# The first stretch of a two-layer decoder trunk: weights cut ahead of x, the first tile's products in two passes, copies of x later

## The chip, the cores and the metric

The kernel runs on one core of a Trainium2 chip. The metric is the device time of one execution in microseconds (us). PE is the engine for matrix products and transposes, DVE the vector engine, ACT the scalar engine, POOL a further vector processor, and SP a queue that only issues transfers (DMAs) here. SBUF is the working memory; PE writes its results to PSUM, in banks of 128 x 512 floats.

## What is computed

The reference is a decoder trunk of two layers on 512 positions of width 1024. Layer 0 normalises x, projects it to queries, keys, values and three convolution inputs at once, evaluates a sliding-window attention beside a short gated convolution, and projects both back. Layer 1 has a chunked gated linear attention in its place. Each layer then has a gated feed-forward block with a convolution of width 3, and a gated per-layer embedding. What matters here is the very first step:

```python
h = _rms_norm(x, mix_norm[i])                       # x is 512 x 1024
q, k, v, cb, cc, cx = _split(h @ w_in, HY_SPLITS)   # k and v: 128 columns each
```

Everything is float32. The root mean square is a factor per position, so the kernel projects x times the gain first and multiplies by that factor afterwards.

## The kernel before, in words

**Three products for one.** PE multiplies in a rounded 32-bit format. To keep float32 accuracy, each operand is cut into a high part (rounded) and a low part (the rest), and a product is taken as high x high + high x low + low x high. For x, `split` (line 104) makes the parts: ACT writes the high part a0 with the gain multiplied in (L112), and DVE the low part a1 (L113). For weights, `cut` (line 126) does it: ACT writes wh (L142), DVE wl (L143). `mm3` (line 158) issues the three products: L162 (x high with wh), L163 (x high with wl), L164 (x low with wh).

**Input.** `mixer0` (line 422) loads x in four chunks of 256 columns, each as two transfers `xin[0]` and `xin[1]` (256 positions each), and behind each chunk the matching 256 rows of the key and value weights (`kvr`, 256 columns). All twelve transfers are issued by SP in this order (L433, L433, L434, and again), of 256 KB each. Transfers share eight semaphores, so SP issues the later ones when earlier ones have landed. The weights of the queries (L119) follow on the same queue.

**Order of the first stretch.** x arrives with positions on the partitions, but the products need columns there. So each chunk c is turned by PE: eight transposes of 128 x 128 (L460) into two PSUM tiles `ps`, one for each column tile 2c and 2c+1. `features(c)` does this, then splits both tiles (L112, L113), cuts the chunk's weights (L142, L143), and copies both tiles to `xT` in SBUF, the first on ACT, the second on DVE (L471). `keys_values(k)` multiplies column tile k with the weights: for each of four position blocks the three products of `mm3`, 12 products of 256 columns. They sum up over k = 0..7 in two PSUM tiles `pkv`. In the block under `tc.manual_schedule` PE, DVE and ACT take their instructions in the order in which the program writes them; outside it a scheduler orders them.

The program order is: features(0), keys_values(0), features(1), keys_values(1), features(2), keys_values(2), features(3), keys_values(3) to (7). In `features`, chunk 0 cuts its weights between its two tiles, and the others behind both:

```python
    if m == (c > 0) + 2 * c:
        wkv.append(self.cut(kvr[:, 2 * c : 2 * c + 2, :], "a"))
```

The weights of chunk c (two column tiles) are read by tiles 2c and 2c+1. There are four `ps` tiles; chunk c+2 takes those of chunk c, once all that reads them (split and copies) is done.

**Fills.** `idle(n)` (line 194) issues n products of ones into a PSUM tile that nobody reads (L198). Seven run at the start in `setup`, eight between the transposes of chunk 0 and the first products: `features(0, 8)`.

**Gains.** The gains of the norm arrive as rows and are turned by PE into a column (`vec0`, L222), in the middle of chunk 0's transposes; DVE copies it (L223), and L112 and L113 read it.

**Behind the stretch.** The squares of x for the norm (L486, ACT), the tables of the rotary embedding (from L373 on, DVE), and the query products (L162 to L164 into `ps`, 512 columns) follow.

Of the kernel before, what the change touches and what calls it, by code (L numbers as in the profile page):

```python
# [21 lines left out]
NT = S // P  # L22
ND = D // P
# [33 lines left out]
class Kernel:  # L57
# [364 lines left out]
    def mixer0(self):  # L422
        nc, a, tc = self.nc, self.a, self.tc
        with tc.tile_pool(name="m0", bufs=1) as mp:
# [3 lines left out]
            kvr = self.raw(ND, 256)  # L428
# [10 lines left out]
            xg = self.xg = []  # L439
            tok = lambda k, t: (xg[k][0][:, t * P : (t + 1) * P], xg[k][1][:, t * P : (t + 1) * P])  # L440
            pkv = [self.pa() for _ in range(2)]
            pkv = [pkv[t // 2][:, (t % 2) * 256 : (t % 2) * 256 + 256] for t in range(NT)]
            wkv = []

            def keys_values(k):
                for t in range(NT):
                    self.mm3(
                        pkv[t], tok(k, t), wkv[k // 2](k % 2, 0, 256),
                        start=k == 0 and t % 2 == 0, stop=k == ND - 1 and t % 2 == 1,
                    )  # L450

            def features(c, fill=0):
                ms = (2 * c, 2 * c + 1)
                pss = [self.ps() for _ in ms]
                for u in range(2):
                    if c == 0 and u == 1:
                        self.vec0()
                    for m, ps in zip(ms, pss):
                        for t in (2 * u, 2 * u + 1):
                            nc.tensor.transpose(  # L460
                                ps[:, t * P : (t + 1) * P], xin[u][:, t % 2, m * P : (m + 1) * P], self.ident
                            )
                self.idle(fill)
                for m, ps in zip(ms, pss):
                    hl = self.pair(self.fp, "a0", "a1")
                    self.split(hl, ps, self.g_mix[0][:, m : m + 1])
                    xg.append(hl)
                    if m == (c > 0) + 2 * c:
                        wkv.append(self.cut(kvr[:, 2 * c : 2 * c + 2, :], "a"))
                return [  # L470
                    copy(self.xT[m], ps) for m, ps, copy in zip(ms, pss, (nc.scalar.copy, nc.vector.tensor_copy))  # L471
                ]

            with tc.manual_schedule(engines={ET.PE, ET.DVE, ET.Activation}):
                features(0, 8)
                for c in range(1, 4):
                    keys_values(c - 1)
                    last = features(c)
                for k in range(3, ND):
                    keys_values(k)  # L480
            wq = [self.weights(w_in[:, k0 : k0 + 4, :512], 4, 512, by="a") for k0 in (0, 4)]
            sums = self.few(NT, "ss")
# [174 lines left out]
            pss = {}  # L657
# [101 lines left out]
    def operand(self, m, gain, tags):  # L759


        nc, fp = self.nc, self.mlp
        H = S // 2
        if m % 2 == 0:
            self.scratch = self.four(fp, F32)
        x = self.scratch[:, m % 2]
        nc.scalar.activation(x, self.xT[m], AF.Copy, scale=gain[:, m : m + 1])
        self.xg.append(self.pair(self.fp, *tags))
        self.split(self.xg[m], x)
        if m % 2:  # L770
            e, o, s12, s34 = (self.scratch[:, u] for u in range(4))
            nc.vector.tensor_tensor(s12[:, :H], e[:, H:], o[:, H:], ALU.add)
            nc.vector.tensor_tensor(s12[:, H:], s12[:, :H], e[:, :H], ALU.subtract)
            out = self.four(fp)
            self.split((out[:, 0], out[:, 1]), s12)
            nc.vector.tensor_tensor(s34[:, :H], e[:, :H], e[:, H:], ALU.subtract)
            nc.vector.tensor_tensor(s34[:, H:], o[:, :H], s12[:, H:], ALU.subtract)
            self.split((out[:, 2], out[:, 3]), s34)
            self.forms.append([(out[:, q, c], out[:, q + 1, c]) for q in (0, 2) for c in (slice(0, H), slice(H, S))])
        self.squares(m)  # L780
# [1164 lines left out]
```

## Time and profile before

| what | value |
|---|---|
| time before, median of three runs | 1213.49 us |
| its three runs | 1211.59, 1214.13, 1213.49 us |
| the profiled execution's own time | 1211.17 us |
| its span, first to last instruction | 1209.4 us |
| PE busy | 1201.5 us, 99% of the span |
| DVE, ACT busy | 967.9 and 664.9 us |

A profile is one execution, recorded by the hardware; times in it count from the start of its span. "Busy" is the time in which an engine had an instruction in work. The products on PE are pipelined: one that is recorded with 0.28 us can be followed by the next after 0.12 us, so the distance between two starts is what one costs. PEld is the loading of the stationary operand, which overlaps PE. A row of the timeline has its start, its duration, engine, line, operation, output<-inputs, sizes and count; in brackets stands how long the engine was idle before it, and whom it waited for. In a table of windows the number in brackets is the count of instructions that run in the window, those that reach into it from before among them.

### The profile page before, as it was taken

What the parts mean: (1) busy time and instruction counts of PE and PEld (TensorE: products, weight loads), DVE (VectorE), ACT (ScalarE), POOL (GpSimd) and SP (SyncE); (2) the same over time, 40 slices, a digit from 0 to 9 for tenths busy, and PEclk for the clock granted to TensorE, in tenths of its full rate; (3) what the DMA queues carried; (4) which work ended last, traced back from release to release, by engine and by line L of the source; (5) the groups of instructions that cost most, each with busy time, mean ns of one, the idle gap of its engine ahead of it and who ended that gap; (6) DMA issues with size and microseconds to landing.
All of it is one profiled execution on the core that took longest, in us unless ns stands there. A gap on an engine that the chain in (4) does not pass through costs nothing.

```text
span 1209.4 us, 17733 instructions
## 1 busy us (share of the span) xinstructions
PE 1201.5 (99%) x7030; PEld 1039.7 (86%) x7030; DVE 967.9 (80%) x1529; ACT 664.9 (55%) x1082; POOL 44.5 (4%) x64
## 2 busy tenths in 40 slices
PE   9999999999999999999999999999999999999998
PEld 8877788999899889888988988889998899888877
DVE  6786587899898996746679876687999999978595
ACT  7466465656555644534563555555565555645364
POOL 2600000000000000000100000000000000000000
PEclk9999999999999999999999999999999999999999
DMA  7221322323323242222322222323242424323501
GB/s 221 74 96 43 92 86 70 127 83 105 105 95 115 89 138 97 96 91 91 114 93 70 71 71 70 105 67 108 71 140 70 140 70 131 122 88 106 200 1 70
DMA packets 111271, 117.61 MB, mean 97 GB/s; under 512 B 2856, under 2 KB 106466, under 8 KB 111188
## 3 DMA queue, kind: packets, MB, share of 16 engines
q1 hardware_dynamic: 109824, 115.35, 29.3%
q8 instruction: 55, 0.90, 0.3%
q0 software_dynamic: 560, 0.42, 0.3%
q10 hardware_dynamic: 804, 0.70, 0.2%
q14 instruction: 28, 0.23, 0.1%
HBM read 114.37 MB, written 2.10 MB: 96 GB/s over the span
## 4 chain that ended last, share of the span: by engine, by line
PE 88%; DVE 7%; ACT 2%; issue 1%; POOL 1%; DVEq 0%; ACTq 0%; POOLq 0%
PE ps L162 12%; PE ps L163 12%; PE ps L164 12%; PE pa L163 7%; PE pa L162 7%; PE pa L164 7%; PE ps L848 6%; PE ps L850 5%; PE ps L849 5%; PE pa L848 2%; PE pa L850 2%; PE pa L849 2%; DVE wl L143 1%; PE ps L1345 1%; PE ps L1347 1%
## 5 line engine op out<-in xcount | busy, mean ns | idle before, releaser
L142 ACT ACTIVATE wh<-raw 128x1024 fp32r<-128x1024 f32 (+4 forms) x154 | 152.3, 991 | 152.4 <-PE ps L163 109.3
L143 DVE TENSOR_TENSOR wl<-raw,wh 128x1024 fp32r<-128x1024 f32 (+4 forms) x154 | 175.3, 1140 | 52.9 <-ACT wh L142 52.6
L795 ACT ACTIVATE wh<-raw 128x1024 fp32r<-128x1024 f32 x78 | 82.8, 1061 | 118.3 <-DVE raw L820 65.4
L908 DVE SCALAR_TENSOR_TENSOR zt<-z,vfa,zt 128x510 f32<-128x510 f32 (+1 forms) x176 | 130.9, 746 | 11.7 <-ACT zt L906 11.2
L796 DVE TENSOR_TENSOR wl<-raw,wh 128x1024 fp32r<-128x1024 f32 x78 | 95.4, 1223 | 20.0 <-ACT wh L795 19.9
L906 ACT ACTIVATE zt<-z,vfb 128x512 f32<-128x512 f32 x88 | 71.0, 809 | 29.5 <-DVE four L959 12.8
L162 PE MATMUL ps<-b,wh 128*128 128x512 f32 x192 | 76.8, 400 | 0.0
L163 PE MATMUL ps<-b,wh 128*128 128x512 f32 x192 | 75.2, 392 | 0.0
L164 PE MATMUL ps<-b,wl 128*128 128x512 f32 x192 | 75.0, 391 | 0.0
L163 PE MATMUL pa<-b,wh 128*128 128x512 f32 x176 | 69.0, 392 | 0.0
L163 PE MATMUL pa<-a,wh 128*128 128x512 f32 x176 | 69.0, 392 | 0.0
L162 PE MATMUL pa<-a,wh 128*128 128x512 f32 x176 | 69.0, 392 | 0.0
L162 PE MATMUL pa<-b,wh 128*128 128x512 f32 x176 | 69.0, 392 | 0.0
L164 PE MATMUL pa<-a,wl 128*128 128x512 f32 x176 | 68.5, 389 | 0.0
L164 PE MATMUL pa<-b,wl 128*128 128x512 f32 x176 | 68.5, 389 | 0.0
L848 PE MATMUL ps<-four,wh 128*128 128x256 f32 x232 | 65.2, 281 | 0.4 <-ACT ps L869 0.4
L850 PE MATMUL ps<-four,wl 128*128 128x256 f32 x232 | 64.4, 278 | 0.0
L849 PE MATMUL ps<-four,wh 128*128 128x256 f32 x232 | 64.3, 277 | 0.0
L162 PE MATMUL ps<-a,wh 128*128 128x512 f32 x160 | 63.1, 394 | 0.0
L163 PE MATMUL ps<-a,wh 128*128 128x512 f32 x160 | 62.7, 392 | 0.0
L164 PE MATMUL ps<-a,wl 128*128 128x512 f32 x160 | 62.5, 391 | 0.0
L162 PE MATMUL ps<-uh,wh 128*128 128x512 f32 x128 | 50.3, 393 | 0.0
(469 smaller groups left out, 3504.9 us busy)
## 6 DMA issues: line engine op xcount, KB each, us to landing
raw<-in_ffn_w_up_dram SPq DMA_DIRECT2D x44, 1024.0 KB, 5.0
raw<-in_ffn_w_down_dram SPq DMA_DIRECT2D x13, 1024.0 KB, 4.8
raw<-in_hy_w_in_dram SPq DMA_DIRECT2D x8, 1024.0 KB, 5.1
raw<-in_gla_w_in_dram SPq DMA_DIRECT2D x8, 1024.0 KB, 5.2
raw<-in_ffn_w_down_dram SPq DMA_DIRECT2D x8, 768.0 KB, 4.2
raw<-in_ple_w_gate_dram SPq DMA_DIRECT2D x6, 1024.0 KB, 4.9
raw<-in_hy_w_out_dram SPq DMA_DIRECT2D x16, 256.0 KB, 3.9
raw<-in_gla_w_out_dram SPq DMA_DIRECT2D x4, 1024.0 KB, 4.7
```

The costliest lines, as they stand in the source:

```text
L142: nc.scalar.activation(hv, v, AF.Copy)
L143: nc.vector.tensor_tensor(lv, v, hv.bitcast(F32), ALU.subtract)
L162: mm(out, lh, rh, start=start, stop=False, **kw)
L163: mm(out, lh, rl, start=False, stop=False, **kw)
L164: mm(out, ll, rh, start=False, stop=stop, **kw)
L795: nc.scalar.activation(h, src, AF.Copy)
L796: nc.vector.tensor_tensor(l, src, h.bitcast(F32), ALU.subtract)
L848: mm(out, wh, xh, start=first and j == 0, stop=False, **kw)
L849: mm(out, wh, xl, start=False, stop=False, **kw)
L850: mm(out, wl, xh, start=False, stop=j == ND // 2 - 1, **kw)
L906: nc.scalar.activation(y, z, AF.Identity, scale=w2[:, f : f + 1], bias=bb[:, f : f + 1])
L908: nc.vector.scalar_tensor_tensor(out=y[:, tap:], in0=z[:, : S - tap], scalar=w[:, f : f + 1], in1=y[:, tap:], op0=ALU.mult, op1=ALU.add,)
```

## The change

The order inside the first stretch is written anew. `features` is gone; its parts are now four small functions, and tile 0 has products of its own:

```diff
-            def features(c, fill=0):
-                ms = (2 * c, 2 * c + 1)
-                pss = [self.ps() for _ in ms]
+            def first_keys_values():
+                mm = nc.tensor.matmul
+                wh, wl = wkv[0](0, 0, 256)
+                for t in range(NT):
+                    xh, _ = tok(0, t)
+                    mm(pkv[t], xh, wh, start=t % 2 == 0, stop=False)
+                    mm(pkv[t], xh, wl, start=False, stop=False)
+                for t in range(NT):
+                    mm(pkv[t], tok(0, t)[1], wh, start=False, stop=False)
+
+            def turned_in(c):
+                pss = [self.ps() for _ in range(2)]
                 for u in range(2):
                     if c == 0 and u == 1:
                         self.vec0()
...
-                self.idle(fill)
-                for m, ps in zip(ms, pss):
-                    hl = self.pair(self.fp, "a0", "a1")
-                    self.split(hl, ps, self.g_mix[0][:, m : m + 1])
-                    xg.append(hl)
-                    if m == (c > 0) + 2 * c:
-                        wkv.append(self.cut(kvr[:, 2 * c : 2 * c + 2, :], "a"))
+                return pss
+
+            def weight(c):
+                wkv.append(self.cut(kvr[:, 2 * c : 2 * c + 2, :], "a"))
+
+            def operand(m, ps):
+                hl = self.pair(self.fp, "a0", "a1")
+                self.split(hl, ps, self.g_mix[0][:, m : m + 1])
+                xg.append(hl)
+
+            def keep(c, pss):
                 return [
-                    copy(self.xT[m], ps) for m, ps, copy in zip(ms, pss, (nc.scalar.copy, nc.vector.tensor_copy))
+                    copy(self.xT[2 * c + u], pss[u]) for u, copy in enumerate((nc.scalar.copy, nc.vector.tensor_copy))
                 ]
 
             with tc.manual_schedule(engines={ET.PE, ET.DVE, ET.Activation}):
-                features(0, 8)
+                pss = turned_in(0)
+                self.idle(3)
+                weight(0)
+                for u in range(2):
+                    operand(u, pss[u])
+                first_keys_values()
                 for c in range(1, 4):
-                    keys_values(c - 1)
-                    last = features(c)
-                for k in range(3, ND):
+                    ahead = turned_in(c)
+                    keep(c - 1, pss)
+                    pss = ahead
+                    operand(2 * c, pss[0])
+                    weight(c)
+                    operand(2 * c + 1, pss[1])
+                    keys_values(c)
+                last = keep(3, pss)
+                for k in range(4, ND):
                     keys_values(k)
```

What it does, in the order of the instructions:

- Three fills stand behind chunk 0's transposes, where there were eight.
- On ACT and DVE the weights of chunk 0 are cut ahead of both x tiles of the chunk; before, they stood between the two.
- Tile 0's products come in two passes: for all four position blocks the two with a0, then for all four the one with a1. Before, the three products of a block stood together.
- For chunks 1 to 3 the weights are cut between the chunk's two x tiles; before, they stood behind both.
- The copies of x to `xT` of chunk c stand behind the transposes of chunk c+1 in the program, and ahead of its splits. On ACT and DVE that is behind chunk c's splits and cuts and ahead of chunk c+1's, the place that they had; those of chunk 3 stand behind its products.
- PE's order of transposes and products by tiles is that of before: chunk 0, tile 0, chunk 1, tile 1, chunk 2, tile 2, chunk 3, tiles 3 to 7.

More of the change, by code (lines that the diff above doesn't have):

```diff
@@ L457, in features @@
                         self.vec0()
-                    for m, ps in zip(ms, pss):
+                    for m, ps in zip((2 * c, 2 * c + 1), pss):
                         for t in (2 * u, 2 * u + 1):
@@ L462, in features @@
                             )
-                self.idle(fill)
-                for m, ps in zip(ms, pss):
-                    hl = self.pair(self.fp, "a0", "a1")
-                    self.split(hl, ps, self.g_mix[0][:, m : m + 1])
-                    xg.append(hl)
-                    if m == (c > 0) + 2 * c:
-                        wkv.append(self.cut(kvr[:, 2 * c : 2 * c + 2, :], "a"))
+                return pss
[6 more added lines that the diff above has]
+            def keep(c, pss):
                 return [
-                    copy(self.xT[m], ps) for m, ps, copy in zip(ms, pss, (nc.scalar.copy, nc.vector.tensor_copy))
+                    copy(self.xT[2 * c + u], pss[u]) for u, copy in enumerate((nc.scalar.copy, nc.vector.tensor_copy))
                 ]
             with tc.manual_schedule(engines={ET.PE, ET.DVE, ET.Activation}):
-                features(0, 8)
-                for c in range(1, 4):
-                    keys_values(c - 1)
-                    last = features(c)
-                for k in range(3, ND):
+                pss = turned_in(0)
[4 more added lines that the diff above has]
+                first_keys_values()
+                for c in range(1, 4):
+                    ahead = turned_in(c)
[7 more added lines that the diff above has]
+                for k in range(4, ND):
                     keys_values(k)
```

## The prediction

> **What bounds the kernel now.** I read the page first, then the waits of PE, then the first 45 us by windows, and last the timeline of PE, ACT, DVE and SP there. The page's busy line and the waits of PE (engine, line, what it waited for; us in total, times, longest):
>
> ```profile
> span 1209.4 us, 17733 instructions
> ...
> PE 1201.5 (99%) x7030; PEld 1039.7 (86%) x7030; DVE 967.9 (80%) x1529; ACT 664.9 (55%) x1082; POOL 44.5 (4%) x64
> ```
>
> ```profile
> PE pa L198 <- DVE mhalf L186: 1.3, 1, 1.3
> PE pa L163 <- DVE wl L1325: 0.9, 1, 0.9
> PE ps L1345 <- ACT so L1389: 0.5, 1, 0.5
> PE pa L629 <- ACT pT L637: 0.5, 1, 0.5
> PE ps L848 <- ACT ps L869: 0.4, 2, 0.2
> PE ps L162 <- DVE kT L1532: 0.2, 1, 0.2
> PE pa L163 <- DVE wl L143: 0.2, 1, 0.2
> ```
>
> PE is busy 99% of the span and waits 4.0 us in all, so the time is the length of PE's own list. A cut counts if it takes instructions off that list or ends a hole in it early on, and if what follows really moves up. But busy isn't useful: the change is about the stretch up to 23.1 us, and there PE also runs L198, products of ones whose result nobody reads. PE's timeline of the start (start, us, ..., count):
>
> ```profile
> 1.32 3.36 PE L198 MATMUL pa<-ones_r 128*128 128x512 f32 x7 [1.32 <-DVE mhalf L186]
> 4.47 1.06 PE L460 MATMUL ps<-cf,xin 128*128 128x128 f32 x4
> 5.46 0.28 PE L222 MATMUL pa<-cf,vrow 16*128 16x16 f32 x1
> 5.67 0.97 PE L460 MATMUL ps<-cf,xin 128*128 128x128 f32 x4
> 6.40 2.08 PE L198 MATMUL pa<-ones_r 128*128 128x512 f32 x8
> 8.31 0.28 PE L162 MATMUL pa<-wh,a 128*128 128x256 f32 x1
> 8.53 0.39 PE L163 MATMUL pa<-wl,a 128*128 128x256 f32 x1
> 8.75 0.28 PE L164 MATMUL pa<-wh,a 128*128 128x256 f32 x1
> ```
>
> Start to start, the first seven fills take (4.47-1.32)/7 = 0.45 us each, the eight from 6.40 on (8.31-6.40)/8 = 0.24: PE's clock doubles at about 6.4, although the granted clock reads 1.00 from the start (I take that for missing records). The same stretch by windows (stretch and length, PE busy and count, PEld, DVE, ACT, POOL, PEclk, DMA):
>
> ```profile
> 8.30:9.94 1.64, 1.64 (x13) 1.42 (x12) 1.43 (x3) 0.36 (x1) 0.00 (x0) 1.00 1.07 374
> 9.94:10.73 0.79, 0.79 (x10) 0.79 (x9) 0.00 (x0) 0.00 (x0) 0.00 (x0) 1.00 1.09 385
> 10.73:12.25 1.52, 1.52 (x15) 1.52 (x14) 0.73 (x2) 1.45 (x3) 0.19 (x2) 1.00 1.09 398
> 13.04:14.98 1.94, 1.76 (x15) 1.57 (x14) 1.94 (x4) 1.89 (x5) 1.94 (x4) 1.00 0.83 287
> 15.77:23.14 7.37, 7.37 (x63) 7.24 (x61) 5.51 (x9) 7.27 (x12) 2.96 (x6) 1.00 0.69 157
> 23.14:45.20 22.06, 22.06 (x98) 18.21 (x98) 14.31 (x40) 11.72 (x23) 6.58 (x6) 1.00 0.38 116
> ```
>
> The list reads: products of tile 0 (1.64), transposes of chunk 1 (0.79), tile 1 (1.52), transposes of chunk 2 (0.79, to 13.04), tile 2 (1.94), transposes of chunk 3, then tiles 3 to 7 (7.37). Twelve products cost 1.52 when nothing holds them; tile 2's row has 0.42 more: the wait for wl, below.
>
> **The change part by part.** PE's order stays, transposes of chunk c and then products of tile c, but for five fills fewer and tile 0's inner order; behind 23.1 us PE, POOL and SP have the same lists as before, DVE and ACT swap a few neighbours up to about 33 us. So there are two places to price.
>
> *Five fills off, and the weights ahead of x.* ACT and DVE at the start (idle before, and its releaser, in brackets), and SP's tenth and eleventh transfers:
>
> ```profile
> 6.40 0.69 ACT L112 ACTIVATE a<-ps,vec 128x512 fp32r<-128x512 f32 x1 [3.17 <-PE ps L460]
> 6.99 0.62 ACT L142 ACTIVATE wh<-raw 128x512 fp32r<-128x512 f32 x1
> 7.51 0.68 ACT L112 ACTIVATE a<-ps,vec 128x512 fp32r<-128x512 f32 x1
> 8.08 0.58 ACT L471 COPY xT<-ps 128x512 f32<-128x512 f32 x1
> ```
>
> ```profile
> 7.12 0.75 DVE L113 SCALAR_TENSOR_TENSOR a<-ps,vec,a 128x512 fp32r<-128x512 f32 x1 [1.17 <-ACT a L112]
> 7.79 0.68 DVE L143 TENSOR_TENSOR wl<-raw,wh 128x512 fp32r<-128x512 f32 x1
> ```
>
> ```profile
> 5.84 0.47 SPq L433 DMA_DIRECT2D xin<-in_x_dram  x1
> ```
>
> The fills run until 8.31, but the operand a0 is done at 6.40+0.69 = 7.09, so they hold PE back; the second product starts at 8.53 since wl is done only at 7.79+0.68 = 8.47. In the changed order wh goes first on ACT and adds a wait there, for the first weight transfer; the x operands stand behind it. SP's transfer at 5.84 waits, by the program, for the lane of that weight transfer, so it had landed by 5.84. Then wh runs 5.88 to 6.50; a product operand follows a wh after 0.52 (6.99 to 7.51), so at 6.40: ACT is ready when x is, and the move costs nothing. Its cover is 0.0 us wide, though: each us that the weights land later delays a0 by as much. wl on DVE runs 6.52 to 7.20, a1 at 7.12 as before. Three fills end at 6.40 + 3 x 0.24 = 7.12. So the first product starts at about 7.2 with wh and wl both there, and twelve products (1.5; the four with a1 stand last, a1 is done at 7.87) bring chunk 1's transposes to 8.7 instead of 9.94: **1.25 us** less. From both sides: 1.19 if only the five fills count (5 x 0.24), 1.35 if the first product starts at 7.10.
>
> *wl of the second weight chunk.* PE around 13.04, and what led there on ACT and DVE:
>
> ```profile
> 13.04 0.36 PE L162 MATMUL pa<-wh,a 128*128 128x256 f32 x1
> 13.58 0.39 PE L163 MATMUL pa<-wl,a 128*128 128x256 f32 x1 [0.17 <-DVE wl L143]
> ```
>
> ```profile
> 10.80 1.27 ACT L112 ACTIVATE a<-ps,vec 128x512 fp32r<-128x512 f32 x2 [2.14 <-PE ps L460]
> 11.95 0.64 ACT L142 ACTIVATE wh<-raw 128x512 fp32r<-128x512 f32 x1
> ```
>
> ```profile
> 11.52 1.41 DVE L113 SCALAR_TENSOR_TENSOR a<-ps,vec,a 128x512 fp32r<-128x512 f32 x2 [1.79 <-ACT a L112]
> 12.84 0.68 DVE L143 TENSOR_TENSOR wl<-raw,wh 128x512 fp32r<-128x512 f32 x1
> 13.44 0.68 DVE L471 COPY xT<-ps 128x512 f32<-128x512 f32 x1
> ```
>
> Now wl is third on DVE (two a1, 11.52 to 12.84) and ends at 13.52; PE stands until 13.58. Afterwards it is second. By the same steps from the transposes' start T = 8.7: first operand at T + 0.86 (9.94 to 10.80), wh 0.59 later, a1 at T + 1.58, wl 0.67 behind it, done at T + 2.93 = 11.6. PE asks for it at T + 0.79 + 1.52 + 0.79 + 0.2 = 12.0. It is there 0.4 us early, so the wait goes: **0.42 us** (1.94 - 1.52). If that margin is eaten, up to 0.42 comes back.
>
> *What is late next.* The copies of x now stand behind the next transposes in the list; on ACT and DVE they land between operands. Chunk 3's transposes write the tile that the copy of chunk 1 frees: by the steps above that copy ends on DVE at 12.9, asked for at 13.5. The third chunk's wl ends near 14.2, asked for at 15.7; the fourth's near 16.7, asked for at 18.6. All cover, so I cost these at 0; if the nearest failed, it would cost some 0.1 to 0.4. Chunk 1's x must be there at 8.7; SP's 5.84 row has the weight transfer ahead of it done, and its two pieces of 256 KB, at 0.7 us each (374 GB/s in the 8.30 window), then land near 7.3. The next weights (L119) start when DVE has cut the last chunk, so some 1.9 us earlier; nobody loses a place in SP's or POOL's queue.
>
> *Sum.* 1.25 + 0.42 = 1.7 us. Behind 23.1 PE is full (22.06 of 22.06), and the waits from there on are 2.5 us in five rows, each behind work that PE itself began; so the 1.7 us passes to the end, with ACT's and DVE's room there as the cover. At worst, if a chain fixed in time ended last, all of it would be lost; below that I see nothing, since no later list grows.
>
> The profiled execution took 1211.17 us (span 1209.4 and 1.8 around it): 1209.5 after. The three runs lie 0.4 to 3.0 above it, their median 2.3. Off the median 1213.49 the sum gives 1211.8, off the mean of the four executions (1212.6) 1210.9. I take the middle, 1211.4.
>
> **The rivals.** *The clock doubles earlier.* In a run where it opens near 4.5, the eight transposes from 4.47 take about half as long and before gains 0.9: its a0, wh, wl then bring products at 7.5. The changed kernel has wh no earlier than 5.84 and a0 behind it at 6.40, as now. The head start shrinks from 1.25 to 0.3, and with 0.42 the gain is 0.7: 1212.4. For it: the runs differ by 2.5 us, and one record cannot tell where the clock opens. A later opening changes little, as products then run slow in the fills' place.
>
> *Given back later.* ACT and DVE move up less than PE (ACT is busy 7.27 of 7.37 us in the row of 15.77), and a wait behind 23.1 grows by what PE won: 1213. Against: from 23.14 to 45.20 ACT is busy 11.7 of 22.1 us and DVE 14.3, with room to catch up before the attention.
>
> *Slower: the clock stays shut.* The fills may be what opens it. With three instead of eight, and operands that come a little late, PE might run the products at the slow rate until a later opening; each us so run loses half a us (0.45 against 0.24). The gain is gone if it opens 3.4 us behind the first product, at 10.6; at 15.4 us the net is +2.4: 1215.5. Against: in the trace it opens at about 6.4, ahead of the first fill that goes, and the list has no hole over 0.1 us behind it. [...]
>
> **How the numbers follow.** Chances: 0.68 that the 1.7 us shows, 0.14 for 0.7, 0.11 for given back, 0.07 for slower. About 0.2% (2.4 us, 1211.1) is what a measurement of this kernel can tell from no change; 1.7 us lies inside it, and the runs' scatter and the base decide: of the 0.68 some 0.41 falls below 1211.1, of the 0.14 some 0.03. Faster 0.44, same 0.50, slower 0.06. The range goes from the lowest run less 1.7 and 0.5 for scatter, 1209.4, to the highest (1214.13) less 0.7, 1213.4; the slower case is left out.
>
> **What would show it.** Right: three fills from about 6.4, first product at 7.2, chunk 1's transposes at 8.7, no wait of PE on wl before 23 us, and the products' end at 21.4 instead of 23.14; each later stage 1.7 us earlier. Wrong: a0 on ACT behind 6.5 (weights late), a wait on wl at tile 2, products 0.21 us apart (clock shut), or a PE wait behind 23 us that is longer by what was won.

## The result, and the profile after

| | before | after |
|---|---|---|
| median of 20 runs each | 1211.92 us | 1209.94 us |
| lowest to highest | 1210.40 to 1214.53 | 1209.26 to 1211.01 |
| the profiled execution | 1211.17 | 1209.60 |
| its span | 1209.4 | 1207.8 |

The ratio of after to before is 0.9982, 95% interval 0.9976 to 0.9987: faster by 0.18%, or 1.6 to 2.9 us. It is a real gain, and a little under the 0.2% that the prediction took for its bound.

The busy line and PE's waits of the page and trace after:

```profile
span 1207.8 us, 17724 instructions
...
PE 1199.9 (99%) x7025; PEld 1038.0 (86%) x7025; DVE 968.9 (80%) x1529; ACT 665.2 (55%) x1082; POOL 43.8 (4%) x64
```

```profile
PE pa L198 <- DVE mhalf L186: 1.3, 1, 1.3
PE pa L163 <- DVE wl L1349: 0.9, 1, 0.9
PE pa L653 <- ACT pT L661: 0.5, 1, 0.5
PE ps L1369 <- ACT so L1413: 0.5, 1, 0.5
PE ps L872 <- ACT ps L893: 0.5, 2, 0.3
PE ps L162 <- DVE kT L1556: 0.2, 1, 0.2
```

PE is as full as before, with 5 instructions and 1.6 us less. The wait on wl of L143 is gone, and no later wait took its place (line numbers behind the change are 24 higher). PE's timeline of the start:

```profile
4.47 1.06 PE L469 MATMUL ps<-cf,xin 128*128 128x128 f32 x4
5.45 0.28 PE L222 MATMUL pa<-cf,vrow 16*128 16x16 f32 x1
5.67 0.81 PE L469 MATMUL ps<-cf,xin 128*128 128x128 f32 x4
6.23 0.94 PE L198 MATMUL pa<-ones_r 128*128 128x512 f32 x3
7.04 0.39 PE L457 MATMUL pa<-wh,a 128*128 128x256 f32 x1
7.26 0.28 PE L458 MATMUL pa<-wl,a 128*128 128x256 f32 x1
```

ACT and DVE in the same stretch:

```profile
5.37 0.63 ACT L142 ACTIVATE wh<-raw 128x512 fp32r<-128x512 f32 x1 [2.14 <-DMA raw<-in_hy_w_in_dram]
6.29 1.27 ACT L112 ACTIVATE a<-ps,vec 128x512 fp32r<-128x512 f32 x2 [0.29 <-PE ps L469]
7.80 0.59 ACT L484 COPY xT<-ps 128x512 f32<-128x512 f32 x1 [0.24 <-DVE a L113]
```

```profile
6.03 0.69 DVE L143 TENSOR_TENSOR wl<-raw,wh 128x512 fp32r<-128x512 f32 x1
7.01 1.41 DVE L113 SCALAR_TENSOR_TENSOR a<-ps,vec,a 128x512 fp32r<-128x512 f32 x2 [0.29 <-ACT a L112]
```

ACT cuts the weights while PE still turns x; its next idle time ends with PE, so x and not the weights holds a0. The fills are over at about the time at which a0 is done (6.29 + 0.69 = 6.98), and both parts of the weights have been ready since 6.72. The windows after, cut at the same places of the list:

```profile
7.03:8.58 1.55, 1.55 (x13) 1.55 (x13) 1.55 (x3) 1.12 (x2) 0.00 (x0) 1.00 0.97 291
8.58:9.37 0.79, 0.79 (x10) 0.79 (x9) 0.44 (x1) 0.00 (x0) 0.00 (x0) 1.00 1.06 371
9.37:10.88 1.51, 1.51 (x15) 1.51 (x14) 0.72 (x2) 1.44 (x3) 0.00 (x0) 1.00 1.09 375
11.67:13.18 1.51, 1.51 (x15) 1.51 (x14) 1.51 (x3) 1.46 (x4) 1.29 (x7) 1.00 1.07 414
13.97:21.33 7.36, 7.36 (x63) 7.23 (x61) 6.31 (x10) 7.02 (x12) 4.59 (x9) 1.00 0.82 196
```

Chunk 1's transposes start at 8.58 instead of 9.94, tile 2 takes 1.51 instead of 1.94, and the stretch ends at 21.33 instead of 23.14: 1.81 us less.

### The profile page after: what moved, and what is told of

Its sections match the earlier page's. It is cut to its first block, busy times and chain, and to the rows that moved or that the text cites. A ratio compares the mean times of both kernels' runs of the same rounds, so it can differ in the third digit from the quotient of the medians.

```text
span 1207.8 us, 17724 instructions
## 1 busy us (share of the span) xinstructions
PE 1199.9 (99%) x7025; PEld 1038.0 (86%) x7025; DVE 968.9 (80%) x1529; ACT 665.2 (55%) x1082; POOL 43.8 (4%) x64
## 4 chain that ended last, share of the span: by engine, by line
PE 85%; DVE 9%; ACT 2%; issue 1%; DMA 1%; POOL 1%; ACTq 0%; DVEq 0%; POOLq 0%
PE ps L162 12%; PE ps L163 12%; PE ps L164 12%; PE pa L163 6%; PE pa L162 6%; PE pa L164 6%; PE ps L872 5%; PE ps L874 5%; PE ps L873 5%; PE pa L872 2%; PE pa L874 2%; PE pa L873 2%; DVE wl L143 2%; PE ps L1369 1%; PE ps L1371 1%
## 5 line engine op out<-in xcount | busy, mean ns | idle before, releaser
L143 DVE TENSOR_TENSOR wl<-raw,wh 128x1024 fp32r<-128x1024 f32 (+4 forms) x154 | 175.8, 1142 | 49.6 <-ACT wh L142 49.1
```

The costliest lines, as they stand in the source:

```text
L143: nc.vector.tensor_tensor(lv, v, hv.bitcast(F32), ALU.subtract)
```

## The experiments

The theory: the gain is a head start of some 1.25 us that needs the fills off and the weights ahead together, and 0.42 us of a wait for wl at tile 2; both pass through to the end. The rivals: each fill is worth its own length; the order on ACT and DVE alone is the gain; the clock needs the fills; what is won is given back later.

Two things move the traces by more than some of these effects. One is the moment at which PE's clock doubles (in e7 products of 256 columns start 0.21 us apart ahead of it and 0.12 behind), which differs from run to run; the column "clock" is the first record of the full clock in each trace. The other is the part behind 23 us. So the comparisons use places in the list. All in us; "c1" is the start of chunk 1's transposes, "c2 to c3" the distance from chunk 2's to chunk 3's (transposes and tile 2), "end" the transpose of the positions (L375), the first instruction behind the key and value products, and "rest" the time from there to the start of the last product. The times given below for e1 to e10 are medians of eleven runs each.

| kernel | clock | first product | c1 | c2 to c3 | end | rest |
|---|---|---|---|---|---|---|
| before | 6.36 | 8.31 | 9.94 | 2.74 | 23.15 | 1182.4 |
| before again (e11) | 6.49 | 8.37 | 9.94 | 2.76 | 23.15 | 1182.3 |
| before again (e12) | 7.29 | 8.77 | 10.19 | 2.74 | 23.39 | 1182.3 |
| after | 6.02 | 7.04 | 8.59 | 2.30 | 21.34 | 1182.6 |
| after again (e10) | 6.84 | 7.40 | 8.83 | 2.30 | 21.58 | 1182.5 |
| e1, three fills only | 4.55 | 6.93 | 9.23 | 2.76 | 22.45 | 1182.2 |
| e2, weights first only | 4.58 | 7.55 | 8.98 | 2.75 | 22.19 | 1183.0 |
| e3, wl late again | 4.35 | 6.87 | 8.44 | 2.74 | 21.64 | 1182.5 |
| e4, one pass | 5.71 | 6.89 | 8.98 | 2.31 | 21.75 | 1182.2 |
| e5, eight fills | 6.60 | 8.45 | 9.88 | 2.30 | 22.63 | 1183.1 |
| e6, no fills behind chunk 0 | 4.61 | 6.86 | 8.41 | 2.31 | 21.19 | 1183.4 |
| e7, no fills at the start | 9.05 | 7.52 | 9.64 | 2.31 | 22.41 | 1182.4 |
| e8, five at the start | 7.41 | 7.47 | 8.91 | 2.30 | 21.66 | 1182.5 |
| e9, six at the start, one later | 4.42 | 6.83 | 8.41 | 2.30 | 21.17 | 1182.3 |

**e1, fills alone.**

```diff
-                features(0, 8)
+                features(0, 3)
```

> The order of before with three fills instead of eight. My theory: the fills only covered the wait for the first weights. The first product then waits for wh (6.99 + 0.62 = 7.6 us) and the second for wl (8.47 us), so chunk 1's transposes still start at 9.85 to 9.95 us, tile 2's wait for wl stays, and the time is that of before (ratio 0.9999 to 1.0001). Rival, each fill is worth its own length: five fills less give 1.2 us, transposes at 8.8 us, ratio 0.999. Rival, the fills hold the clock open: products at 0.21 us each and later than before.

Measured: 1211.04 us, ratio 0.9996 (0.9987 to 1.0005). PE at its first products, and the DVE row that ends the wait:

```profile
5.61 0.94 PE L198 MATMUL pa<-ones_r 128*128 128x512 f32 x3
6.93 0.38 PE L162 MATMUL pa<-wh,a 128*128 128x256 f32 x1 [0.38 <-ACT wh L142]
7.80 0.39 PE L163 MATMUL pa<-wl,a 128*128 128x256 f32 x1 [0.49 <-DVE wl L143]
```

```profile
7.07 0.68 DVE L143 TENSOR_TENSOR wl<-raw,wh 128x512 fp32r<-128x512 f32 x1
```

and ACT ahead of it:

```profile
5.68 0.69 ACT L112 ACTIVATE a<-ps,vec 128x512 fp32r<-128x512 f32 x1 [2.45 <-PE ps L460]
6.26 0.62 ACT L142 ACTIVATE wh<-raw 128x512 fp32r<-128x512 f32 x1
```

The fills' place is taken by waits, first for wh and then for wl, so the fills covered them. The times expected were those of a late clock; here it opened at 4.55, x was turned sooner, and the whole chain with it. Eight fills from 5.61 on, of 0.24 each (e2 has them from 5.62 to 7.55), would have ended near 7.5, still ahead of the 7.80 at which wl lets the second product go: so with an early clock the kernel before should stand at 9.23 and 22.45 too. No run of before had an early clock, so that is worked out and not measured. The times alone do not exclude the 0.999 of the rival that prices each fill at its length, since the interval begins at 0.9987; the waits in the trace speak against it.

**e2, weights first alone.**

```diff
+                if c == 0:
+                    wkv.append(self.cut(kvr[:, :2, :], "a"))
                 for m, ps in zip(ms, pss):
...
-                    if m == (c > 0) + 2 * c:
+                    if c and m == 1 + 2 * c:
```

> The order of before with the first weights cut ahead of both x tiles, and all eight fills. My theory: the eight fills hold PE until 8.3 us whatever is ready, so only the short wait of the second product goes: transposes of chunk 1 at 9.8 us, 0.1 us won, ratio 0.9999. Rival, the order on ACT and DVE is the whole gain: transposes at 8.7 us, ratio 0.999.

Measured: 1211.43 us, ratio 1.0 (0.9991 to 1.0009).

```profile
5.62 2.09 PE L198 MATMUL pa<-ones_r 128*128 128x512 f32 x8
7.55 0.28 PE L162 MATMUL pa<-wh,a 128*128 128x256 f32 x1
7.67 0.28 PE L163 MATMUL pa<-wl,a 128*128 128x256 f32 x1
```

No product waits, but the fills last until 7.55. The 9.8 us expected for c1 was that of a late clock; against e1, where it opened as early, c1 is 0.25 earlier. With the same early clock e6, which has the weights first, the two passes and no fills, reaches its first product at 6.86 and c1 at 8.41, 0.57 earlier than e2 and 0.82 earlier than e1. So neither half brings the head start alone; both single-cause rivals fall in the traces. The 0.57 needs the two passes as well: e4 below has the weights first, three fills and one pass, DVE starts its a1 as early as in e6 (6.87 in both), and its c1 is that of e2, 8.98.

**e3, the later weights behind both x tiles again** (chunks 1 to 3).

```diff
                     operand(2 * c, pss[0])
-                    weight(c)
                     operand(2 * c + 1, pss[1])
+                    weight(c)
```

> The changed kernel with the weights of chunks 1 to 3 behind both x tiles again. My theory: the wait of tile 2's second product on wl comes back, 0.35 to 0.45 us, tile 2 takes 1.9 us instead of 1.5, and the query products start that much later than in the changed kernel; about 0.4 us of its gain is lost (ratio to before 0.9985 instead of 0.9982, inside the noise of the times). Rival, the wait was not on the path: nothing moves behind tile 2.

Measured: 1209.69 us, ratio 0.9986 (0.9978 to 0.9995), in the times not to be told from the change. In the trace the wait is back:

```profile
11.54 0.36 PE L162 MATMUL pa<-wh,a 128*128 128x256 f32 x1
12.07 0.39 PE L163 MATMUL pa<-wl,a 128*128 128x256 f32 x1 [0.17 <-DVE wl L143]
```

The distance of starts is 0.53 where the change has 0.20 at that place, c2 to c3 is 2.74 against 2.30, and the end stands at 21.64; e6, with nearly the same clock and c1, ends at 21.19. The 0.44 us is on PE's list and stays there.

**e4, tile 0 in one pass.**

```diff
-                first_keys_values()
+                keys_values(0)
```

> The changed kernel with tile 0's products in one pass, three for each block as before. My theory: the third product waits for a1, done on DVE at 7.77 us, instead of starting at 7.38; with the restart of the pipeline chunk 1's transposes start 0.4 to 0.55 us later than in the changed kernel (9.0 to 9.15 us instead of 8.59), and stay so to the end of the stretch. Rival, the two passes are worth nothing, because the weights ahead already make all three ready: transposes at 8.6 us.

Measured: 1209.95 us, ratio 0.9986 (0.9977 to 0.9995).

```profile
7.12 0.28 PE L163 MATMUL pa<-wl,a 128*128 128x256 f32 x1
7.68 0.39 PE L164 MATMUL pa<-wh,a 128*128 128x256 f32 x1 [0.28 <-DVE a L113]
```

The third product waits for a1, as expected: 0.56 us from start to start where the two passes have 0.12. From first product to c1 it takes 2.09 us against 1.55 in the change. The two passes are worth 0.5 us, a part of the head start that the prediction had inside its 1.5 for twelve products.

**e5, eight fills in the changed order.**

```diff
-                self.idle(3)
+                self.idle(8)
```

> The changed kernel with eight fills again. My theory: PE is held until 8.2 to 8.3 us, so the first product starts there and chunk 1's transposes at 9.7 to 9.8; of the 1.2 us of head start 1.15 is lost, the 0.42 us at tile 2 stays: ratio to before about 0.9995. Rival, fills behind chunk 0 cost nothing: as the changed kernel.

Measured: 1210.92 us, ratio 0.9996 (0.9987 to 1.0005). Against the changed kernel with nearly the same clock (e10) the first product is 1.05 later, and the end 1.05 too: once the weights are ahead, five fills cost nearly their length (0.25 each here, eight from 6.44 to 8.45, so 1.26).

**e6, no fills behind chunk 0.**

```diff
-                self.idle(3)
+                self.idle(0)
```

> The changed kernel with no fill at all behind chunk 0's transposes. My theory: the first product waits for a0 at 7.0 to 7.1 us anyway, so PE stands idle for 0.7 us and nothing else moves: same times of all later stages, within 0.1 us. Rival, the fills keep the clock open: the products cost 0.21 us instead of 0.12 for a while and the stretch ends 0.5 us or more later.

Measured: 1210.05 us, ratio 0.9990 (0.9981 to 0.9999).

```profile
5.23 0.65 PE L469 MATMUL ps<-cf,xin 128*128 128x128 f32 x4
6.86 0.39 PE L457 MATMUL pa<-wh,a 128*128 128x256 f32 x1 [0.97 <-ACT a L112]
7.08 0.31 PE L458 MATMUL pa<-wl,a 128*128 128x256 f32 x1
```

PE stands 0.97 us, and from the third on the products start 0.12 us apart (7.23, 7.34, 7.46 and on), the fast rate, as in the change (7.38, 7.50, 7.62). e3, with three fills and as early a clock, has its first product at 6.87: these three fills do nothing here. But the clock had opened at 4.61, ahead of the place of the fills, so this trace cannot say what they do while it is still shut. What a0 waits for here is wh, ahead of it on ACT, and wh for its transfer:

```profile
5.60 0.63 ACT L142 ACTIVATE wh<-raw 128x512 fp32r<-128x512 f32 x1 [2.37 <-DMA raw<-in_hy_w_in_dram]
6.13 1.25 ACT L112 ACTIVATE a<-ps,vec 128x512 fp32r<-128x512 f32 x2
```

**e7, no fills at the start.**

```diff
-            self.idle(7)
+            self.idle(0)
```

> The changed kernel without the seven fills of the start (three stay behind chunk 0). PE then begins with transposes when x is there, at about 3.9 us instead of 4.47. [...]

Measured: 1210.56 us, ratio 0.9994 (0.9985 to 1.0003).

```profile
4.09 1.09 PE L469 MATMUL ps<-cf,xin 128*128 128x128 f32 x4 [4.09 <-DMA xin<-in_x_dram]
...
7.52 0.41 PE L457 MATMUL pa<-wh,a 128*128 128x256 f32 x1
7.73 0.41 PE L458 MATMUL pa<-wl,a 128*128 128x256 f32 x1
...
8.80 0.40 PE L457 MATMUL pa<-wh,a 128*128 128x256 f32 x1
9.01 0.30 PE L458 MATMUL pa<-wl,a 128*128 128x256 f32 x1
9.16 0.65 PE L460 MATMUL pa<-wh,a 128*128 128x256 f32 x4
```

Here the rival mechanism of the shut clock is seen at work: the products follow at 0.21 us until 9.05 and at 0.12 behind. c1 is at 9.64, 0.8 later than with an opening at 6.84 (e10). Without the fills at the start the clock opened 1.8 us later than in any trace of the kernels with all seven (7.29), in this one run. Counted from PE's first work, at 4.09, that is 5.0 us.

**e8 and e9, fewer fills at the start.**

```diff
-            self.idle(7)
+            self.idle(5)      # e8; in e9 6, and idle(1) behind chunk 0
```

> The changed kernel with five fills at the start instead of seven. The x of chunk 0 is there at about 3.9 us and at 4.6, but PE's transposes start at 4.47 because seven fills last so long. My theory: transposes start at 3.9, chunk 0's end about 0.5 us earlier, a0 is then held by wh on ACT (done near 6.0): first product near 6.7 instead of 7.04, 0.2 to 0.4 us won if the clock opens as early as now. Rival, the clock opens later with less work ahead of it, and the gain goes.

> The changed kernel with six fills at the start instead of seven and one behind chunk 0 instead of three. The first x is usable at 4.09 us (seen with five fills), and six fills end at 4.04, so the transposes start at 4.09 without the hole that five left. My theory: the first product starts 0.2 to 0.4 us earlier than in the changed kernel for the same opening of the clock, and the stretch ends as much earlier; in the times that is at most 0.03% and not to be told from the changed kernel. Rival: the clock opens later with less work ahead, and it is slower by 0.3 us or more.

Measured: e8 1209.88 us, ratio 0.9993 (0.9984 to 1.0002; the two medians alone give 0.9987, its runs lie between 1209.57 and 1212.0); e9 1209.37 us, 0.9983 (0.9975 to 0.9992). ACT in e9:

```profile
5.57 0.63 ACT L142 ACTIVATE wh<-raw 128x512 fp32r<-128x512 f32 x1 [2.35 <-DMA raw<-in_hy_w_in_dram]
6.11 1.25 ACT L112 ACTIVATE a<-ps,vec 128x512 fp32r<-128x512 f32 x2
```

The transposes do start at 4.07, but wh then waits for its transfer, a0 stands behind it, and c1 comes at 8.41 as in e6: the expected 0.2 to 0.4 us did not come. This is the wait that the change put on ACT, now the one that ends last. In e8 the clock opened at 7.41, so slow fills held the first product until 7.47, and its theory, for an early clock, stays untested; one run cannot say whether the hole of 0.3 us in front of its transposes had to do with that.

**e10 to e12, both kernels again.**

> The changed kernel once more. My theory: the clock opens at another time, since that moved between 4.35 and 6.6 us in the runs so far; if it opens near 4.5, the first product starts near 6.85 and the query products' stretch (the transpose of the positions) begins near 21.2 instead of 21.34; the rest is 1182.2 to 1183.4 us long, as in all runs. Rival: the start is as in the first profile, and the scatter of the times is all from behind 23 us.

> The kernel before once more, for another opening of the clock. My theory: with an opening near 4.5 us its chunk 1's transposes start near 9.2 (wl bounds it, as with three fills) and the positions' transpose at 22.4 to 22.5, so that the gain is 1.2 to 1.3 us there and not 0.7 as the first rival had it; with a late one 9.9 to 10.1 and 23.1 to 23.4. Rival, the opening does not matter to it: 23.15 again.

> The kernel before a further time, with the same expectations: positions' transpose at 22.4 to 22.5 us for an early opening of the clock, 23.1 to 23.4 for a late one, and 1182.2 to 1183.4 us from there to the last product.

Measured: e10 1209.35 us, ratio 0.9985 (0.9976 to 0.9994); e11 1211.02 and e12 1211.28, one run each. All three had a late clock, so the early case of before stayed unseen. The later the clock opened, the later the end: 23.15, 23.15 and 23.39 before, 21.34 and 21.58 after. Their means, 23.23 and 21.46, are 1.77 us apart.

*The later stretch.* The rest is 1182.2 to 1183.4 in all kernels, though their lists are alike from 33 us on. The two longest have a wait of PE on a copy of ACT, of e6 and of e5, that no trace of before or after has:

```profile
PE ps L872 <- ACT ps L897: 0.5, 1, 0.5
```

```profile
PE ps L872 <- ACT ps L883: 0.6, 1, 0.6
```

So the first pair of profiles, 1.81 us apart at 21 to 23 us and 1.6 at the end, shows no giving back that could be told from this scatter; three traces of before and two of after have the same rest within 0.4.

## Why the prediction was right, point by point

- *What bounds the kernel:* right. PE stayed full, and what came off its list came off the time.
- *Head start, 1.25 us:* c1 moved by 1.35 in the first pair. Of that 0.17 is the clock, which opened 0.34 earlier and ended chunk 0's transposes sooner (fills from 6.23 instead of 6.40); 1.2 is the change. e1 and e2 show that neither the cut of the fills nor the weights ahead brings it alone, e5 that eight fills take most of it away, and e4 that the two passes carry 0.5 of it. The prediction had counted on the passes (its four products with a1 stand last) without giving them a price of their own.
- *wl of the second chunk, 0.42:* 0.43 by the windows, brought back by e3.
- *The move on ACT at no cost:* right where the clock opened late behind seven fills: in after, e10 and e5 wh starts at 5.37 to 5.43 and a0 waits for PE. Where it opened early it was not: e1, with the weights between the x tiles, starts a0 at 5.68, e2, e3 and e6, with the weights first, at 6.08 to 6.14, right behind a wh that began at 5.54 to 5.61. So the warning about its cover was right: there, and in e9, the transfer is the bound and costs a0 some 0.4 us.
- *Late next:* no wait of PE up to the end of the stretch; wl of the second chunk was done at 10.83 + 0.68 = 11.51 on DVE, asked for at 11.88.

The DVE row behind the last point:

```profile
10.83 0.68 DVE L143 TENSOR_TENSOR wl<-raw,wh 128x512 fp32r<-128x512 f32 x1
```

- *Sum, 1.7 us passing to the end:* 1.77 in the stretch by five traces and 1.5 in the spans (1209.4, 1209.2 and 1209.5 against 1207.8 and 1207.9). The medians of the runs differ by 2.0, both times that both kernels ran in many rounds. Between 1.5 and 2.0 the interval does not decide; the runs of before reach to 1214.5, and no trace caught such a run. What makes them stays open.
- *The base:* the term that was off. The median of the three runs shown, 1213.49, was 1.6 above that of twenty, 1211.92. The sum on the profiled execution alone (1209.5) came out nearer to 1209.94 than the middle taken, 1211.4. The prediction set the bound of what can be told apart at 1211.1, and 1209.94 lies below it; that the change is still under 0.2% comes from the lower time of before beside it. On which side of that bound the result would fall was luck, as the nearly even chances (0.44 and 0.50) say.
- *Rival of the early clock:* the case is frequent (five of the thirteen traces with fills at the start open under 5 us), but its price was wrong. It gave 0.7; e1 stands for before and e6 for after there, 22.45 against 21.19, so 1.26. The step that failed was the products of before at 7.5: a0 started at 5.68 on ACT and wl was done only at 7.75. In the changed kernel a0 did stand behind wh, as this rival had it, but at 6.13 (e6) and not at 6.40.
- *Rival of the shut clock:* products do run slow while the clock is shut (e7), but no trace shows that the cut fills bear on when it opens: with three fills behind chunk 0 it opened at 6.84 (e10), with eight at 7.29 (e12). No trace has a late clock and no fills there. In e1, e2, e3, e6 and e9 the clock opened 3.0 to 3.3 us after PE's first fill. No run shows an opening at 10.6 or 15.4 us, for which the prediction priced this rival: the latest came at 9.05 (e7), and at 7.41 (e8) with fills at the start.

## What to carry to other kernels

Where an engine is full of filler, find out what the filler covers before it is cut: here 0.9 us of waits stood under it (0.38 and 0.49 in e1), and no gain of the cut alone was measured. Put work whose input is already there (the weights) ahead of work that still waits for another engine (x), and check which transfer then becomes the head of that queue. A difference of some tenths of a microsecond is read at a fixed place of the instruction list in several traces, not from run times, and a single record of the clock's opening is no constant (4.35 to 7.29 us with the same seven fills).

## What was not expected of the hardware

PE's clock doubled at very different times in kernels with the same seven fills from 1.32 us on: between 4.35 (e3) and 7.29 us (e12), that is 3.0 to 6.0 us after its first work. One and the same kernel had 6.02 and 6.84 (after and e10), another 6.36, 6.49 and 7.29 (before, e11 and e12). What sets the moment is not shown by these traces.

A change in the moment of opening is worth up to 0.25 us at the end of the stretch among the late openings, and about 0.7 us between early and late in before, if e1 stands for it.
